# A Mamba-2 branch on one core: the skip term through the decay matrix, the diagonal products of two chunks in one run, and a new place for the last four squares

## The chip, the cores and the metric

The kernel runs on one core of a Trainium2 chip. A core has five engines that run their own instruction streams side by side: TensorE (PE) for matrix products, with its weight loads shown apart (PEld), VectorE (DVE), ScalarE (ACT), GpSimd (POOL) and SyncE (SP), which here only issues transfers. They wait for each other through semaphores. The metric is the device time of one execution in microseconds (us); the time of a kernel is the median of its runs.

## What is computed

One layer of a diffusion backbone on 512 latent tokens of width 1024, with 256 context tokens: a modulated norm, one wide projection, a bidirectional Mamba-2 branch and a windowed attention beside it, gates, an output projection, and a gated convolutional feed-forward part. The change lies in the Mamba-2 branch (4 groups of 8 heads of 64, state 128, chunks of 128 tokens) and in what follows it:

```python
# ssd_scan, one direction
cb = jnp.einsum('bclgn,bcsgn->bgcls', cc, bc)
scores = cb[:, :, None] * jnp.exp(segsum(ac))
y_diag = jnp.einsum('bgrcls,bcsgrp->bclgrp', scores, xc)
y_off = jnp.einsum('bclgn,bcgrpn,bgrcl->bclgrp', cc, states[:, :-1], jnp.exp(cs))
# ssd_output
y = y + d_skip.reshape(SSD_GROUPS, SSD_HPG, 1).astype(y.dtype) * xs
return rmsnorm(y.reshape(Bsz, L, D_SSD) * jax.nn.silu(z), g)
```

The forward and the backward scan are added, so each chunk of a group has one 128 x 128 matrix a head for what its own tokens give each other, two products with the states that come from the left and from the right, and a skip term: its inputs times a number for each head and token (the diagonal that the two directions share, and `d_skip`).

## The kernel before

The program is one long list of steps. A runner goes through it and loads each step's weights one step ahead: SP issues the transfer (L177), ACT makes the rounded part (L183) and DVE the rest (L184), and each product of a projection is three passes on PE (L238, L239, L241). Small pieces of other work are put between a projection's passes through a list, BETWEEN. A scheduler settles the static order of each engine from the program; operations that are recorded as kept in program order stay in it, and on POOL that holds for nearly all of them: the helpers `gp` (L1574) and `gs` (L1577) record it.

For each group, `ssd_steps` gives a step for the states and, for each of the chunks c = 0 to 3, `chunk_in` and `chunk_out`:

- *States.* `advance` takes a state one chunk on: a product on PE (L1597), a decay on POOL (`st<-st,eT`), a sum on DVE (L1600). The states from the right are made first, one behind another, and one of them is needed in chunk 0.
- *chunk_in.* The product `cb` (PE L1696); its diagonal `cbd` (DVE L1698); the skip's coefficients `coef` (POOL); for c > 0 two tiles `dg`, the coefficients on a diagonal (POOL). Then the decay matrices E, two tiles of four heads: ACT L1719, L1722 and L1726, DVE L1723; E times `cb` (DVE L1730); and for c > 0 `E + dg` (POOL), by which the skip goes through the same product as the rest.
- *chunk_out.* Two products with the states (PE L1754, eight matmuls, 16 passes in the trace), each scaled into a tile `te` (DVE L1756); the diagonal products (PE L1762, eight matmuls whose results are 64 columns wide, again 16 passes); the forward state's `advance`; and `y`, the sum of the two `te` (POOL). For c = 0 the skip is a product `dx` on POOL, which four transposes on PE (L1778) add to the diagonal products' bank.
- *late.* Some steps later: the next chunk's decays are loaded, `y` gets the diagonal part (DVE L1779), and the gate `zs` is multiplied in (POOL, for chunk 3 DVE L1783). For groups 1 to 3, squares of the group before are summed (ACT L1570, POOL L1571).

The E tiles come from three buffers, the products' banks (`mis`) from a common pool. After the last chunk of a group its four gated tiles are stored (`yz_d`, SP L1798).

Behind group 3 stands the output projection of this branch. `y_split(ks)` reloads rows of `yz_d` (SP L1840), splits each into a rounded part `yh` (ACT L1842) and a rest `yl` (DVE L1843). The first five rows are of earlier groups. The four tiles of group 3 are squared and summed here, in `square(True)`, from a list. One of the projection's weights is held in a tile that is called `yh` as well (its number is 7766 in the rows below; L183 writes it), and so is PE's operand of the last split.

The step list from which this part comes starts with

```python
[([], lambda: (y_split(range(8)), square(True), square(True), y_split([8, 9]), square(True), square(True), y_split([10, 11])))]
```

Of the kernel before, what the change touches and what calls it, by code (L numbers as in the profile page):

```python
# [9 lines left out]
F32 = mybir.dt.float32  # L10
# [3 lines left out]
ALU = mybir.AluOpType  # L14
# [4 lines left out]
P = 128  # L19
# [20 lines left out]
def raw(ap):  # L40
    return ap.bitcast(F32)
# [3 lines left out]
def tile_hybrid_layer(  # L45
# [32 lines left out]
    V, S, G, T = nc.vector, nc.scalar, nc.gpsimd, nc.tensor  # L78
# [3 lines left out]
    hpool = ctx.enter_context(tc.tile_pool(name="hpool", bufs=1))  # L82
# [27 lines left out]
    def misb():  # L110
        return bank("mis")
# [32 lines left out]
    for j, t in enumerate((wdn[0], DSUMS[1], DSUMS[2], DSUMS[5], DSUMS[4], wdn[1], wdn[3])):  # L144
        for u in range(DU):
            n = min(2, DK - 2 * u) * HC
# [99 lines left out]
    ident = cpool.tile([P, P], F32, name="ident")  # L246
# [181 lines left out]
    with tc.tile_pool(name="spool", bufs=1) as sp:  # L428
# [177 lines left out]
        def square(x_, q, n, k, x):  # L606
            sq = B_[x, k] = tmp(("ta", "tb")[k % 2])[:, :n] if k else q
            S.activation(sq, x_[:, k, :], AF.Square)
# [57 lines left out]
        for j in range(KT):  # L666
# [46 lines left out]
            x = ("hi", "lo") if j >= NU else ("hh", "hl")  # L713
# [31 lines left out]
        for n in range(2):  # L745
            for j in range(KT):
                x = ("hi", "lo") if j >= NU else ("hh", "hl")
# [668 lines left out]
    zp = zpool.enter_context(tc.tile_pool(name="zpool", bufs=1, side="right", reuse_waits="tile"))  # L1416
    bp = bpool.enter_context(tc.tile_pool(name="bpool", bufs=1, reuse_waits="tile"))
# [18 lines left out]
    def h8(a):  # L1436
        return a.rearrange("p (h d) -> p h d", h=8)

    def bc64(a):
        return a.unsqueeze(2).to_broadcast([P, 8, 64])  # L1440
# [132 lines left out]
    def gp(*a):  # L1573
        return tc.keep_in_program_order(G.tensor_tensor(*a))  # L1574
# [4 lines left out]
    def ssd_steps(g):  # L1579
        d = GR[g]  # L1580
# [96 lines left out]
        def chunk_in(c):  # L1677

            if not g and not c:
                far_in(0)  # L1680
            fb = []
            for dr in range(2):
                f = bp.tile([P, 8, P], F32, tag="fb", name="fb", bufs=4)
                a = bass.AP(
                    tensor=cs_d.tensor, offset=cs_d.offset + (32 * dr + 8 * g) * L + c * P, ap=[[0, P], [L, 8], [1, P]]
                )
                dma = nc.sync.dma_start(f, a)
                if not g and not c:
                    tc.add_manual_dep(dma.ins, M_LOADS["x", 16].ins.name, QUEUED, reason="decays behind a projection's weights")
                fb.append(f)  # L1690
            d["E"] = []

            def products():
                cb = d["cb"] = misb()
                tok = slice(c * P, (c + 1) * P)
                T.matmul(cb[:, :P], d["BT"][:, tok], d["CT"][:, tok], start=True, stop=True)  # L1696
                cbd = bp.tile([P, 1], F32, tag="cbd", name="cbd", bufs=2)
                V.tensor_tensor_reduce(  # L1698
                    cb[:, P : 2 * P], cb[:, :P], ident, op0=ALU.mult, op1=ALU.add, scale=1.0, scalar=0.0, accum_out=cbd
                )  # L1700
                coef = d["coef"] = bp.tile([P, 8], F32, tag="coef", name="coef", bufs=2)
                gs(coef, TT[:, c, 8 * g : 8 * g + 8], cbd, None, ALU.mult)
                gp(coef, coef, bcs[:, 8 * g : 8 * g + 8], ALU.add)
                d["dg"] = [diagonal(q) for q in range(2)] if c else None

            def diagonal(q):
                dg = bp.tile([P, 4, P], F32, tag="dg", name="dg", bufs=2)
                w = d["coef"][:, 4 * q : 4 * q + 4].unsqueeze(2).to_broadcast([P, 4, P])
                gp(dg, ident.unsqueeze(1).to_broadcast([P, 4, P]), w, ALU.mult)
                return dg  # L1710

            def decays():
                for q in range(2):
                    E = bp.tile([P, 4, P], F32, tag="E", name="E", bufs=3)
                    eb = misb()
                    F4 = fb[0][:, 4 * q : 4 * q + 4, :]
                    for u in range(4):
                        h = 8 * g + 4 * q + u
                        e0 = S.activation(E[:, u, :], F4[:, u, :], AF.Identity, bias=TX[:, c, 0, h : h + 1])  # L1719
                        if u == 0 and c:  # L1720
                            tc.keep_in_program_order(e0)
                        S.activation(eb[:, u * P : (u + 1) * P], fb[1][:, 4 * q + u, :], AF.Identity, bias=TX[:, c, 1, h : h + 1])  # L1722
                    V.copy_predicated(E, sel.unsqueeze(1).to_broadcast([P, 4, P]), eb.rearrange("p (h l) -> p h l", h=4))  # L1723
                    d["E"].append(E)
                for E in d["E"]:
                    S.activation(flat(E), flat(E), AF.Exp)  # L1726

            def weighed():
                for q, E in enumerate(d["E"]):
                    V.tensor_tensor(E, E, d["cb"][:, :P].unsqueeze(1).to_broadcast([P, 4, P]), ALU.mult)  # L1730
                    if c:
                        gp(E, E, d["dg"][q], ALU.add)

            if g in BY_BLOCKS and not c:
                decays()
                BETWEEN[1:2] = [lambda f=BETWEEN[1]: (f(), products(), weighed())]
            else:
                products()
                decays()
                weighed()  # L1740
            if g and c > 1:
                square()
            if g < 3 and c == 3:
                far_in(0, g + 1)

        def chunk_out(c):
            xs, E, far = d["xs"], d["E"], d.pop(("far", c))
            tok = slice(c * P, (c + 1) * P)
            parts = []
            for dr, s in ((0, d["Sf"]), (1, d["Sb"][c])):  # L1750
                ps = misb()
                for ct in range(4):
                    z = slice(ct * P, (ct + 1) * P)
                    T.matmul(ps[:, z], s[:, z], d["CT"][:, tok], start=True, stop=True)  # L1754
                t = tmp("te")
                V.tensor_tensor(t, ps, flat(far[:, dr]), ALU.mult)  # L1756
                parts.append(t)

            yd = misb()
            for h in range(8):  # L1760
                o = yd[64 * (h % 2) : 64 * (h % 2) + 64, (h // 2) * P : (h // 2 + 1) * P]
                T.matmul(o, xs[:, c, h * 64 : (h + 1) * 64], E[h // 4][:, h % 4, :], start=h < 2, stop=c > 0 and h > 5)  # L1762
            dx = None
            if not c:
                dx = zp.tile([P, 512], F32, tag="th", name="dx", bufs=1)
                gp(h8(dx), h8(xs[:, c, :]), bc64(d["coef"]), ALU.mult)
            if c < 3:
                d["Sf"] = advance(d["Sf"], 0, c, weigh_in(0, c))
            y = bp.tile([P, 512], F32, tag="tf", name="y", bufs=1)
            gp(y, parts[0], parts[1], ALU.add)  # L1770

            def late():

                if c < 3:
                    far_in(c + 1)
                for ct in range(0 if c else 4):
                    z = slice(ct * P, (ct + 1) * P)
                    tc.keep_in_program_order(T.matmul(yd[:, z], dx[:, z], ident, start=False, stop=ct == 3, is_transpose=True))  # L1778
                tc.keep_in_program_order(V.tensor_tensor(y, yd, y, ALU.add))  # L1779
                z = d["zt"][:, :, tok]  # L1780
                x = y.rearrange("p (a t) -> p a t", a=4)
                if c == 3:
                    V.tensor_tensor(z, x, z, ALU.mult)  # L1783
                else:
                    gp(z, x, z, ALU.mult)
                if g and c in (0, 3):
                    square()

            assert not BETWEEN
            if g < 3:  # L1790
                BETWEEN.extend([lambda: None] * 4 + [lambda: (late(), turn(1)), turn])
            else:
                BETWEEN.extend([lambda: None] * 2 + [late])
# [43 lines left out]
    def y_split(ks):  # L1837
        for k in ks:
            t = tmp("ta" if k < 3 else "tc") if k < 5 else ldt[k % 3] if k % 6 < 3 else cp.tile([P, L], F32, tag="ld", name="ld", bufs=3)
            nc.sync.dma_start(t, yz_d[k])  # L1840
            h, l = yh[k // 4][:, k % 4, :], yl[k // 4][:, k % 4, :]
            S.activation(h, t, AF.Copy, scale=col(V_SG, k))  # L1842
            V.scalar_tensor_tensor(l, t, col(V_SG, k), raw(h), ALU.mult, ALU.subtract)  # L1843
# [462 lines left out]
    def down_step(j, u):  # L2306
# [36 lines left out]
        return [("dn", DU * j + u + n) for n in range(4 if tail else 1)], fn  # L2343

    run(
        [([], lambda: (y_split(range(8)), square(True), square(True), y_split([8, 9]), square(True), square(True), y_split([10, 11])))]
        + fill[n3:]
        + [([], zpool.close), os_first(0), ([], lambda: y_split(range(12, 16))), os_first(1)]
        + [os_step(2)]
# [96 lines left out]
```

## Time and profile before

| | |
|---|---|
| median of 3 runs | 1215.3 us (1214.98 to 1215.76) |
| profiled execution | 1215.35 us, its span 1213.6 us |
| granted clock of PE | 0.999 |
| PE | 1203.6 us busy, 99% |
| DVE | 918.6 us, 76% |
| ACT | 684.4 us, 56% |
| POOL | 263.8 us, 22% |

Group 0's four chunks begin near 440 us, group 3's near 667 us, and the first split of a reloaded row is at 722 us. A row of a timeline gives the start, the length, the engine, the line, the operation with the tiles that it writes and reads, how many instructions the row holds, and in brackets how long the engine had been idle before it and what it then waited for. A row of the chain gives the start, the share of time that this piece had on the chain, and its engine and line. A row of waits gives the engine and line that waited, for what, the total in us, how often, and the longest.

### The profile page before, as it was taken

The numbers are of one execution on the slowest core, as the hardware profiler recorded it, in microseconds if no ns is written. First come the engines' busy times: TensorE is split into PE (matmuls) and PEld (weight loads), VectorE is DVE, ScalarE is ACT, GpSimd is POOL, SyncE is SP. The second block draws the span as 40 slices with busy tenths as digits, with TensorE's granted clock in tenths as the row PEclk, the third lists the DMA queues.
The fourth block names the chain that finished last, engine by engine and source line by source line (L and its number), as shares of the span: only waits on it lengthen the run. The fifth ranks groups of instructions, "written<-read, shape, count | busy, mean of one in ns | idle before, by whom it ended". The sixth has DMA issues, their size and how long they took to land.

```text
span 1213.6 us, 17847 instructions
## 1 busy us (share of the span) xinstructions
PE 1203.6 (99%) x6429; PEld 1005.6 (83%) x6429; DVE 918.6 (76%) x1476; ACT 684.4 (56%) x1269; POOL 263.8 (22%) x274
## 2 busy tenths in 40 slices
PE   9999999999999999999999999999999999999998
PEld 6798888888878878788787887888988888888886
DVE  4857887888565588788887978677677767668787
ACT  4557887778543467476575664223544343436654
POOL 0000121100102546264382762000200100110021
PEclk9999999999999999999999999999999999999999
DMA  9655889844747737566477668687266634437662
GB/s 367 253 148 185 161 229 271 170 133 139 170 140 240 228 113 199 157 162 192 145 178 264 176 228 265 221 251 242 50 163 148 195 117 138 130 107 226 213 185 97
DMA packets 129417, 224.30 MB, mean 185 GB/s; under 512 B 27336, under 2 KB 70640, under 8 KB 129328
## 3 DMA queue, kind: packets, MB, share of 16 engines
q1 hardware_dynamic: 115248, 195.61, 52.0%
q0 software_dynamic: 13792, 27.27, 10.1%
q8 instruction: 51, 0.84, 0.3%
q14 instruction: 38, 0.31, 0.1%
q10 hardware_dynamic: 288, 0.27, 0.1%
HBM read 196.17 MB, written 45.02 MB: 199 GB/s over the span
## 4 chain that ended last, share of the span: by engine, by line
PE 90%; DMA 3%; DVE 2%; POOL 2%; issue 1%; ACT 1%; SPq 0%; DVEq 0%; POOLq 0%; ACTq 0%
PE acc L241 18%; PE acc L238 18%; PE acc L239 18%; PE score L979 3%; PE po L1028 3%; PE pt L1015 2%; PE mis L582 2%; PE mis L1754 2%; PE mis L1597 2%; PE mis L2304 2%; PE mis L2302 2%; PE mis L2303 2%; DMA xs_d<-xb 1%; PE acc L2304 1%; PE acc L2302 1%
## 5 line engine op out<-in xcount | busy, mean ns | idle before, releaser
L184 DVE TENSOR_TENSOR wlo<-wraw,whi 128x1024 fp32r<-128x1024 f32 (+1 forms) x115 | 148.3, 1289 | 89.2 <-ACT whi L183 88.3
L183 ACT CAST whi<-wraw 128x1024 fp32r<-128x1024 f32 (+1 forms) x115 | 120.2, 1046 | 154.2 <-PE acc L239 103.4
L238 PE MATMUL acc<-hlh,whi 128*128 128x512 f32 x472 | 192.8, 409 | 0.0
L241 PE MATMUL acc<-hlh,wlo 128*128 128x512 f32 x472 | 185.6, 393 | 0.0
L239 PE MATMUL acc<-hll,whi 128*128 128x512 f32 x472 | 185.0, 392 | 0.0
L238 PE MATMUL acc<-mh,whi 128*128 128x512 f32 x368 | 143.3, 389 | 0.0
L239 PE MATMUL acc<-ml,whi 128*128 128x512 f32 x368 | 143.2, 389 | 0.0
L241 PE MATMUL acc<-mh,wlo 128*128 128x512 f32 x368 | 143.2, 389 | 0.0
L241 PEld LDWEIGHTS acc<-hlh,wlo 128*128 128x128 f32 x472 | 88.6, 188 | 19.9 <-issue 0.5
L238 PEld LDWEIGHTS acc<-hlh,whi 128*128 128x128 f32 x472 | 88.8, 188 | 17.6 <-issue 2.8
L239 PEld LDWEIGHTS acc<-hll,whi 128*128 128x128 f32 x472 | 88.9, 188 | 17.4 <-issue 2.2
L238 PEld LDWEIGHTS acc<-mh,whi 128*128 128x128 f32 x368 | 69.1, 188 | 14.4
L241 PEld LDWEIGHTS acc<-mh,wlo 128*128 128x128 f32 x368 | 69.1, 188 | 14.3
L239 PEld LDWEIGHTS acc<-ml,whi 128*128 128x128 f32 x368 | 69.1, 188 | 14.2
L164 POOL DMA_DIRECT2D dsum<-wdn x24 | 25.3, 1118 | 194.3 <-DVE wlo L1112 183.7
L988 DVE CUSTOM_DVE_ANT_0 p<-score,winm,nsink 128x512 f32<-128x512 f32 (+1 forms) x64 | 51.8, 810 | 15.3 <-PE score L979 13.8
L995 ACT ACTIVATE p<-p,mneg 128x512 f32<-128x512 f32 (+1 forms) x64 | 49.7, 777 | 15.4 <-DVE mneg L988 14.9
L813 DVE SCALAR_TENSOR_TENSOR tm<-wraw,csil,tm 128x512 f32<-128x512 f32 x56 | 45.9, 819 | 13.1 <-DMA wraw<-wm 12.4
L1023 DVE TENSOR_TENSOR ptl<-pt,pth 128x512 fp32r<-128x512 f32 x72 | 47.5, 685 | 8.4 <-ACT pth L1019 7.7
L238 PE MATMUL acc<-hch,whi 128*128 128x256 f32 x176 | 53.2, 302 | 0.0
L1112 DVE TENSOR_TENSOR wlo<-wraw,whi 128x1024 fp32r<-128x1024 f32 x30 | 36.7, 1223 | 18.3 <-ACT whi L1109 18.2
L241 PE MATMUL acc<-hch,wlo 128*128 128x256 f32 x176 | 49.8, 283 | 0.0
(458 smaller groups left out, 3054.3 us busy)
## 6 DMA issues: line engine op xcount, KB each, us to landing
wraw<-wup SPq DMA_DIRECT2D x44, 512.0 KB, 4.0
dsum<-wdn POOLq DMA_DIRECT2D x24, 704.0 KB, 8.7
wraw<-wm SPq DMA_DIRECT2D x32, 512.0 KB, 4.1
fb<-cs_d SPq DMA_DIRECT2D x32, 512.0 KB, 7.5
wraw<-wx SPq DMA_DIRECT2D x24, 512.0 KB, 4.1
wm<-wm SPq DMA_DIRECT2D x16, 512.0 KB, 7.9
wraw<-wz SPq DMA_DIRECT2D x16, 512.0 KB, 4.7
far<-us_d SPq DMA_DIRECT2D x32, 256.0 KB, 5.1
```

What stands on the lines that cost most here:

```text
L183: F["cast"] = S.copy(hi[:, :n], r[:, :n])
L184: F["sub"] = V.tensor_tensor(lo[:, :n], r[:, :n], raw(hi[:, :n]), ALU.subtract)
L238: T.matmul(ps, wh, xh[:, k0 + k, :], start=a, stop=False)
L239: T.matmul(ps, wh, xl[:, k0 + k, :], start=False, stop=False)
L241: T.matmul(ps, wl, xh[:, k0 + k, :], start=False, stop=b)
L813: V.scalar_tensor_tensor(acc, r[:, u * 512 : u * 512 + 512], sc, acc, ALU.mult, ALU.add)
L988: V.tensor_tensor_reduce(p[:, :w], d["ps"][i][:, o0 : o0 + w], m, op0=ALU.add, op1=ALU.min, scale=1.0, scalar=nsink[:, h : h + 1], accum_o ...
L995: S.activation(p, p, AF.Exp, bias=d["mneg"][:, i : i + 1], scale=-1.0, accum_out=d["den"][:, i : i + 1])
L1023: V.tensor_tensor(d["ptl"][x], d["pt"][x], raw(d["pth"][x]), ALU.subtract)
L1112: sum_step(V.tensor_tensor(d["w"][1], d["r"], raw(d["w"][0]), ALU.subtract), 1 + (4 <= g < 12))
L2302: T.matmul(ps, h, wh, start=st, stop=False, skip_group_check=True)
L2304: T.matmul(ps, h, wl, start=False, stop=en, skip_group_check=True)
```

## The change

The skip of chunk 0 goes the way of the others: `dg` and `E + dg` are made for every chunk, and `dx` and the four transposes of L1778 are gone. The diagonal products of chunk 0, and in groups 0 to 2 also of chunk 2, are not done in their own `chunk_out`, but in the next chunk's, in one run of sixteen matmuls with that chunk's own. Since a held chunk's E lives longer, an odd chunk's second E tile comes from another pool, and a held chunk's `y` too. The sum of `y` and the gate's product are then done for both chunks in the later one's `late`. In group 3, chunks 2 and 3 keep a run each. The last four squares, which stood two by two between the splits of rows 8 to 11, now all stand behind the first five splits.

```diff
-                d["dg"] = [diagonal(q) for q in range(2)] if c else None
+                d["dg"] = [diagonal(q) for q in range(2)]
...
-                    E = bp.tile([P, 4, P], F32, tag="E", name="E", bufs=3)
+                    if c % 2 and q:
+                        E = hpool.tile([P, 4, P], F32, tag="rbc4", name="E")
+                    else:
+                        E = bp.tile([P, 4, P], F32, tag="E", name="E", bufs=3)
...
-                    if c:
-                        gp(E, E, d["dg"][q], ALU.add)
+                    gp(E, E, d["dg"][q], ALU.add)
...
-            yd = misb()
-            for h in range(8):
-                o = yd[64 * (h % 2) : 64 * (h % 2) + 64, (h // 2) * P : (h // 2 + 1) * P]
-                T.matmul(o, xs[:, c, h * 64 : (h + 1) * 64], E[h // 4][:, h % 4, :], start=h < 2, stop=c > 0 and h > 5)
-            dx = None
-            if not c:
-                dx = zp.tile([P, 512], F32, tag="th", name="dx", bufs=1)
-                gp(h8(dx), h8(xs[:, c, :]), bc64(d["coef"]), ALU.mult)
+            held = c == 0 or c == 2 and g < 3
+            d.setdefault("held", []).append((c, E))
+            done = []
+            for n, Es in [] if held else d.pop("held"):
+                yd = misb()
+                for h in range(8):
+                    o = yd[64 * (h % 2) : 64 * (h % 2) + 64, (h // 2) * P : (h // 2 + 1) * P]
+                    T.matmul(o, xs[:, n, h * 64 : (h + 1) * 64], Es[h // 4][:, h % 4, :], start=h < 2, stop=h > 5)
+                done.append((n, yd))
...
-            y = bp.tile([P, 512], F32, tag="tf", name="y", bufs=1)
+            y = hpool.tile([P, 512], F32, tag="q2", name="y") if held else bp.tile([P, 512], F32, tag="tf", name="y", bufs=1)
             gp(y, parts[0], parts[1], ALU.add)
+            d["y", c] = y
...
-                for ct in range(0 if c else 4):
-                    z = slice(ct * P, (ct + 1) * P)
-                    tc.keep_in_program_order(T.matmul(yd[:, z], dx[:, z], ident, start=False, stop=ct == 3, is_transpose=True))
-                tc.keep_in_program_order(V.tensor_tensor(y, yd, y, ALU.add))
-                z = d["zt"][:, :, tok]
-                x = y.rearrange("p (a t) -> p a t", a=4)
-                if c == 3:
-                    V.tensor_tensor(z, x, z, ALU.mult)
-                else:
-                    gp(z, x, z, ALU.mult)
+                for n, yd in done:
+                    y = d.pop(("y", n))
+                    tc.keep_in_program_order(V.tensor_tensor(y, yd, y, ALU.add))
+                    z = d["zt"][:, :, n * P : (n + 1) * P]
+                    x = y.rearrange("p (a t) -> p a t", a=4)
+                    if n == 3:
+                        V.tensor_tensor(z, x, z, ALU.mult)
+                    else:
+                        gp(z, x, z, ALU.mult)
...
-        [([], lambda: (y_split(range(8)), square(True), square(True), y_split([8, 9]), square(True), square(True), y_split([10, 11])))]
+        [([], lambda: (y_split(range(5)), [square(True) for _ in range(4)], y_split(range(5, 12))))]
```

The lines behind L1704 move by up to 3 in the changed kernel: L1754 becomes L1756, L1762 becomes L1768, L1779 becomes L1782, L1842 becomes L1845.

The order on POOL, group 3, from chunk 0's coefficients to its `y`, before:

```order
L1577 TENSOR_SCALAR coef<-TT,cbd 128x8
L1574 TENSOR_TENSOR coef<-coef,bcs 128x8
L1574 TENSOR_TENSOR st<-st,eT 128x512 x2
L1574 TENSOR_TENSOR dx<-xs,coef 128x512
L1574 TENSOR_TENSOR st<-st,eT 128x512
L1574 TENSOR_TENSOR y<-te 128x512
```

and now:

```order
L1577 TENSOR_SCALAR coef<-TT,cbd 128x8
L1574 TENSOR_TENSOR coef<-coef,bcs 128x8
L1574 TENSOR_TENSOR dg<-ident,coef 128x512 x2
L1574 TENSOR_TENSOR E<-E,dg 128x512 x2
L1574 TENSOR_TENSOR st<-st,eT 128x512 x3
L1574 TENSOR_TENSOR y<-te 128x512
```

Two `dg` and two sums into E stand ahead of the states, and `dx` is gone. On PE, in the same place, chunk 0's eight products with the states are now four, four projection passes, and four more, and the 64-column run of chunk 0 is gone.

The order on DVE, group 3, between chunk 1 and chunk 2, from chunk 1's two `te` to chunk 2's E (`y` is the sum with the diagonal part, `tm` and `mod` belong to the modulation's small sums, `g1h` to the output gate), before:

```order
L1756 TENSOR_TENSOR te<-mis,far 128x512 x2
L811 TENSOR_SCALAR tm<-wraw,csil 128x512
L1600 TENSOR_TENSOR st<-st,mis 128x512
L1698 ISA mis,cbd<-mis,ident 128x128
L1698 ISA cbd 128x1
L1779 TENSOR_TENSOR y<-mis,y 128x512
L813 SCALAR_TENSOR_TENSOR tm<-wraw,csil,tm 128x512
L1723 COPY_PREDICATED E<-sel,mis 128x512 x2
L813 SCALAR_TENSOR_TENSOR tm<-wraw,csil,tm 128x512
L1730 TENSOR_TENSOR E<-E,mis 128x512 x2
```

and now:

```order
L1758 TENSOR_TENSOR te<-mis,far 128x512 x2
L1782 TENSOR_TENSOR y<-mis,y 128x512 x2
L811 TENSOR_SCALAR tm<-wraw,csil 128x512
L1600 TENSOR_TENSOR st<-st,mis 128x512
L1698 ISA mis,cbd<-mis,ident 128x128
L1698 ISA cbd 128x1
L813 SCALAR_TENSOR_TENSOR tm<-wraw,csil,tm 128x512
L1977 TENSOR_SCALAR g1h<-mod_94 128x8
L813 SCALAR_TENSOR_TENSOR tm<-wraw,csil,tm 128x512
L1726 COPY_PREDICATED E<-sel,mis 128x512 x2
L813 SCALAR_TENSOR_TENSOR tm<-wraw,csil,tm 128x512
L1733 TENSOR_TENSOR E<-E,mis 128x512 x2
```

Both `y` sums stand ahead of the state sum and of chunk 2's `cbd`, and one more `tm` and `g1h` ahead of E.

The order on ACT behind group 3, from the last split of an earlier group's row on (`yh_7766` written by L183 is the second weight of the output projection, `whi` the other weights, `ta` the squares), before:

```order
L1842 ACTIVATE yh_7768<-tc,vec 128x512
L778 ACTIVATE tb<-acc 128x512
L183 CAST whi<-wraw 128x1024
L183 CAST yh_7766<-wraw 128x1024
L1842 ACTIVATE yh_7768<-ld,vec 128x512
L1842 ACTIVATE yh_7768<-ld_7762,vec 128x512
L183 CAST whi<-wraw 128x1024
L1842 ACTIVATE yh_7768<-ld_7763,vec 128x512
L1570 ACTIVATE ta<-zs 128x512 x2
```

and now:

```order
L1845 ACTIVATE yh_7768<-tc,vec 128x512
L778 ACTIVATE tb<-acc 128x512
L1570 ACTIVATE ta<-zs 128x512 x4
L183 CAST whi<-wraw 128x1024
L1845 ACTIVATE yh_7768<-ld,vec 128x512
L183 CAST yh_7766<-wraw 128x1024
L1845 ACTIVATE yh_7768<-ld_7762,vec 128x512
L1845 ACTIVATE yh_7768<-ld_7763,vec 128x512
L1845 ACTIVATE yh_7770<-ld_7764,vec 128x512
```

The four squares stand together behind the earlier groups' splits, and the second weight's cast stands behind the split of the first reloaded row instead of ahead of it.

## The prediction

> **What bounds the kernel now.** I read the shares of busy time first, then the waits of TensorE, then the chain of work that ended last.
>
> ```profile
> span 1213.6 us, 17847 instructions
> PE 1203.6 (99%) x6429; PEld 1005.6 (83%) x6429; DVE 918.6 (76%) x1476; ACT 684.4 (56%) x1269; POOL 263.8 (22%) x274
> PE 90%; DMA 3%; DVE 2%; POOL 2%; issue 1%; ACT 1%; SPq 0%; DVEq 0%; POOLq 0%; ACTq 0%
> PE acc L241 <- DVE wlo L184: 1.3, 1, 1.3
> ```
>
> PE is busy 99% of the span and the chain lies on it for 90%, so a pass taken off PE is time saved, and a wait given to PE is time lost. The last row is PE's longest wait, the only one over 1.0 us. Both sides of the change meet in the stretch where the chain leaves PE:
>
> ```profile
> 671.99 0.23 PE acc L241
> ...
> 681.78 0.45 PE mis L1778 x4
> ...
> 706.66 2.51 POOL E L1574 x2
> 709.17 2.23 POOL ssq L1571
> ...
> 714.80 1.06 DVE zs L1783
> ...
> 719.68 4.06 DMA ld<-yz_d
> ...
> 735.48 1.14 DVE wlo L184
> 736.63 0.04 issue
> 736.67 0.50 PE acc L241
> ```
>
> From 682 to 737 us the chain runs over POOL, DVE, SP and ACT: group 3's decay matrices, the gate, the trip through memory and the row splits, up to the weight for which PE waits. POOL is busy 22% over the span, but in this stretch it is what sets the end.
>
> **What PE saves.** One run of the diagonal products, in group 0:
>
> ```profile
> 440.47 1.95 PE L1754 MATMUL mis<-CT,st 128*128 128x128 f32 x16
> 442.35 1.09 PE L1762 MATMUL mis<-E,xs 128*64 128x128 f32 x16
> 443.38 1.12 PE L1597 MATMUL mis<-xw,Bk 128*128 128x512 f32 x2
> L1754 PE MATMUL mis<-CT,st 128*128 128x128 f32 x256 | 31.2, 275 | 0.0
> L1762 PE MATMUL mis<-E,xs 128*64 128x128 f32 x256 | 17.5, 279 | 0.0
> ```
>
> With one pass at 0.275 us, the last L1754 pass starts at 440.47 + 1.95 - 0.275 = 442.145, so its sixteen are (442.145 - 440.47) / 15 = 0.112 apart; the first L1762 pass comes 0.205 after it, 0.09 more than that spacing. L1762's last pass starts near 443.165 (0.279 before its end), so its sixteen are 0.054 apart, and L1597 comes 0.215 after the last, 0.16 more. Entering and leaving a 64-column run costs **about 0.25 us** in all. The sixteen passes of the second chunk cost the same 0.87 wherever they stand.
>
> The change leaves 9 of the 16 runs: two go in each of groups 0 to 2, one in group 3. The four transposes of L1778 (0.45 in the chain's row) go in every group. Groups 0 to 2: 3 x (0.45 + 2 x 0.25) = **2.85 us saved**. Group 3: 0.45 + 0.25 = 0.70. What the change puts in their place in groups 0 to 2 (two `dg`, two sums into E on POOL, less the product `dx`) I cost at nothing: the products of a held chunk wait for the next chunk's own E, which POOL finishes later than the held one, and between the chunks lie projections on PE. If that cover were gone, one group would lose about 3.5 us of POOL work (2.04 + 2.54 - 1.04, rows below).
>
> **What group 3 loses.** Here the projections between the chunks are few. Times are in the clock of the trace, without the 2.85 us by which all of it comes earlier.
>
> ```profile
> 667.83 1.07 POOL L1574 TENSOR_TENSOR st<-st,eT 128x512 f32<-128x512 f32 x1
> 669.70 1.06 POOL L1574 TENSOR_TENSOR st<-st,eT 128x512 f32<-128x512 f32 x1 [0.80 <-DVE st L1600]
> 670.72 1.04 POOL L1574 TENSOR_TENSOR dx<-xs,coef 128x512 f32<-128x512 f32 x1
> ...
> 678.57 2.04 POOL L1574 TENSOR_TENSOR dg<-ident,coef 128x512 f32<-128x512 f32 x2
> 680.57 2.54 POOL L1574 TENSOR_TENSOR E<-E,dg 128x512 f32<-128x512 f32 x2
> 683.09 1.27 POOL L1574 TENSOR_TENSOR zs<-y,zs 128x512 f32<-128x512 f32 x1
> ...
> 687.93 1.40 POOL L1574 TENSOR_TENSOR y<-te 128x512 f32<-128x512 f32 x1 [0.34 <-DVE te L1756]
> ...
> 689.98 2.49 POOL L1574 TENSOR_TENSOR dg<-ident,coef 128x512 f32<-128x512 f32 x2
> 694.24 3.01 POOL L1574 TENSOR_TENSOR E<-E,dg 128x512 f32<-128x512 f32 x2 [1.76 <-DVE E L1730]
> ...
> 699.49 2.26 POOL L1574 TENSOR_TENSOR zs<-y,zs 128x512 f32<-128x512 f32 x1
> 701.70 1.06 POOL L1574 TENSOR_TENSOR st<-st,eT 128x512 f32<-128x512 f32 x1
> ```
>
> *Chunk 0.* Before, the two state steps start at 667.83, right behind the coefficients. Now the order puts two `dg` and two sums into E ahead of them: 667.9 + 2.04 + 2.54 = 672.5, then state 1.06, DVE's sum (0.68, row below), state 1.06, sum 0.68: about 676.0. PE comes to the run at 672.06, does the first four products (0.9), four projection passes (0.23 each), and wants the last state at 673.9. It **waits about 2.2 us**, between 1.5 (if DVE is quicker) and 3 (if `dg` and E take the 2.49 and 3.01 of the later rows). Nothing hides it: the four passes are all that stands between.
>
> *Chunk 1.* POOL's `y` follows the late products, near 678.7; then coefficients, `dg`, E to about 685.6, against 683.1. The gate product `zs` (1.27) has left this place, so the square sum ends near 687.9, the state at 688.9, and the `y` of chunk 1 at 690.3, against 689.34.
>
> *Chunk 2.* DVE's order now matters:
>
> ```profile
> 688.10 0.68 DVE L1600 TENSOR_TENSOR st<-st,mis 128x512 f32<-128x512 f32 x1
> 688.70 0.28 DVE L1698 CUSTOM_DVE_ANT_0 mis<-mis,ident 128x128 f32<-128x128 f32 x1
> ...
> 689.36 0.69 DVE L1779 TENSOR_TENSOR y<-mis,y 128x512 f32<-128x512 f32 x1 [0.32 <-POOL y L1574]
> ...
> 693.39 1.27 DVE L1730 TENSOR_TENSOR E<-E,mis 128x512 f32<-128x512 f32 x2
> ...
> 696.01 1.26 DVE L1974 TENSOR_SCALAR g1h<-mod 128x8 f32<-128x8 f32 x1
> ```
>
> Before, the sum `y` stood behind the diagonal of chunk 2's product (L1698), and only `y` waited for POOL. Now both `y` sums stand ahead of the state sum and of that diagonal, and queue them behind POOL's `y` at 690.3: sum 0.69, one scaling of 0.5, state sum 0.68, diagonal 0.35, so 692.5 in place of 689.0, **3.5 us later**. From that diagonal to POOL's E it was 694.24 - 689.0 = 5.2. Of these, `y` with its wait (1.0) goes, and `g1h` (1.26) and one more scaling step (0.7) stand in its place: 6.2. POOL's E starts near 698.8, 4.6 later than before.
>
> *Chunk 3.* E 2.5 to 3.0, square sum 2.2, now two `zs` in place of one (1.27 to 2.26 each), state 1.06; from the state's end at 702.76 to the end of chunk 3's E at 709.17 it was 6.4, and these steps keep their order. With E 2.5, one `zs` short and one between, the E of chunk 3 ends near 714.5 (bounds 713 and 716) in place of 709.17.
>
> ```profile
> 708.92 1.09 PE L1762 MATMUL mis<-E,xs 128*64 128x128 f32 x16
> ...
> 723.01 0.39 PE L238 MATMUL acc<-yh,yh 128*128 128x512 f32 x1
> 717.16 1.05 ACT L183 CAST yh<-wraw 128x1024 fp32r<-128x1024 f32 x1
> 722.49 0.72 ACT L1842 ACTIVATE yh<-ld,vec 128x512 fp32r<-128x512 f32 x1 [4.28 <-DMA ld<-yz_d]
> 720.22 1.21 DVE L184 TENSOR_TENSOR yh<-wraw,yh 128x1024 fp32r<-128x1024 f32 x1
> ```
>
> Before, PE takes the second half of chunk 3's run at 708.92 + 8 x 0.054 = 709.4, only 0.2 after POOL has it ready. There was no slack, so from here PE is late by 714.5 - 709.4 = **5.1 us**, whatever it lost at chunk 0 and gained from its own 0.70.
>
> *The row splits.* The second output weight (the `yh` written by L183) was cast at 717.16, before the first reload arrived at 722.45. Now it stands behind the split of that reload. The reload came 13.3 us after chunk 3's E (722.45 - 709.17), along gate, store and load, and these keep their order. So cast 13.3 + 0.7 + 1.05 = 15.05, DVE's part 1.21 more: 16.3. PE wants the first at 723.01 - 709.17 = 13.8 and the second 0.46 later; counted from E it waits 1.25, then 0.8: **2.05 us** new. Against it goes the wait of 1.3 at 736.67: the four squares with their sums on POOL now end before the later splits, which on DVE need no more than their uncontended length. If that cover fails, the 1.3 stays.
>
> **Sum.** -2.85 + 5.1 + 2.05 - 1.3 = **+3.0**. On the profiled execution (1215.35 with what lies around its span, level with the median 1215.3) this is 1218.3. With E's bounds of 713 and 716, it is 1216.8 to 1219.8. The change breaks even where chunk 3's E ends at 711.5.
>
> **Rivals.**
>
> *The slip is swallowed and the saving shows (faster).* If POOL and DVE have enough gaps to bring chunk 3's E in by 709.5, the sum is -2.85 + 2.05 - 1.3 = -2.1, so 1213.2, and without the new wait at the splits -2.85 - 1.3, so 1211.2. For it speaks POOL's idle time in the rows (0.80, 0.34 and 1.76); against it that chunk 0's addition of 3.5 us stands ahead of a state for which PE has four passes of cover, and that the last of the gaps is behind DVE, which is itself moved later. 1211.0 to 1213.5.
>
> *About even.* If the square sum of chunk 1 takes the short length and POOL's `y` ends near 688.9, the diagonal of chunk 2 is 2.1 and not 3.5 later; with both `zs` short, E ends between 711.5 and 713: 1215.3 to 1216.8.
>
> *A longer loss (slower).* The same POOL operations have two lengths in the rows: `dg` 2.04 and 2.49, E 2.54 and 3.01, `zs` 1.27 and 2.26, the long ones beside DVE work from SBUF. If the added ones are all long, chunk 2's E ends at 702.5 and chunk 3's at 702.5 + 2.2 + 2 x 2.26 + 1.06 + 6.4 = 716.7, and the sum gives 1220.5; with the long wait at chunk 0 feeding into it, up to 1222. [...]
>
> *The run's overhead is not a matter of runs.* If the 0.25 belongs to each chunk's products and not to the run, seven runs fewer save nothing: 6 x 0.25 = 1.5 us of the saving goes, 1219.8.
>
> **How the numbers follow.** Forecast 0.50, spread over 1216.8 to 1219.8; even 0.22; faster 0.12; longer loss 0.11; overhead stays 0.05. Predicted 1218.3. About 0.2%, 2.4 us, is what a measurement of this kernel can tell from no change: under 1212.9 is faster, over 1217.7 slower. Slower: two thirds of the forecast (0.34) and the two last rivals, 0.50. Same: the rest of the forecast, the even case and a little of the faster one, 0.39. Faster 0.11. The range of 8 in 10 leaves out the faster case below 1213 and the upper end of the longer loss: 1213.0 to 1221.0.
>
> **What would show it.** In the profile after: no L1778 rows and about 0.45 + 0.5 us less PE time in each of groups 0 to 2, with no new waits there; a PE wait of about 2 us on a state (L1600) in group 3; E of chunk 3 from POOL some 5 us later against the run before it, with a PE wait of 2 to 3 us on it; a wait on the second output weight of about 2 us, and none at the third and fourth. I am wrong if PE does not wait at group 3's last diagonal run, or if the waits arise in groups 0 to 2.

## The result and the profile after

The changed kernel takes 1230.92 us (median of 4 runs, 1229.6 to 1231.95) against 1215.53 us beside it: a ratio of 1.0126, 95% interval 1.0114 to 1.0138. It is 15.4 us slower. The direction was forecast, the size was not: 3 us were forecast, and the range ended at 1221.0. Two executions that took far longer than the others of their kernel (3380.73 us with group 3 alone changed, 1336.17 us of the kernel before) are left out of the ratios below.

The page of the changed kernel, the rows that answer to the first ones of before:

```profile
span 1227.8 us, 17812 instructions
PE 1204.4 (98%) x6413; PEld 1005.8 (82%) x6413; DVE 916.8 (75%) x1476; ACT 685.5 (56%) x1269; POOL 276.5 (23%) x286
PE 82%; DVE 6%; DMA 3%; POOL 3%; ACT 2%; issue 2%; DVEq 0%; POOLq 0%; ACTq 0%; SPq 0%
```

PE's share of the chain fell from 90% to 82%; what it lost went above all to DVE (2% to 6%), the rest to POOL, ACT and issue. POOL has 12.7 us more work. The waits of PE in the changed kernel (what waited, for what; us in total, times, longest):

```profile
PE mis L1768 <- POOL E L1574: 3.9, 3, 2.1
PE mis L1756 <- DVE st L1600: 3.1, 1, 3.1
PE mis L1597 <- ACT xsc L1549: 2.9, 2, 1.7
PE mis L1450 <- DVE tc L1431: 1.5, 3, 0.7
PE mis L1756 <- ACT xsc L1549: 1.2, 1, 1.2
PE mis L1616 <- DVE xw L1585: 1.1, 1, 1.1
...
PE mis L1696 <- DVE te L1758: 0.8, 1, 0.8
PE mis L1756 <- ACT xs L1549: 0.6, 1, 0.6
PE acc L241 <- DVE wlo L184: 0.6, 1, 0.6
PE acc L241 <- DVE yh L184: 0.5, 1, 0.5
```

The first two rows and the last two are group 3 and the row splits, where waits were forecast. Nearly all others lie in groups 0 to 2, where none was. (The wait on `xw` is not the change's: it stands ahead of group 0's first chunk and is 0.4 us in the kernel before, 0.4 to 1.1 in the runs below with five banks.) To split the loss in place, take the first sum of context states in group 3. In the timeline of before it stands at

```profile
656.13 1.88 PE L1616 MATMUL mis<-xw,Bkc 128*128 128x512 f32 x4
```

and in that of the changed kernel at

```profile
662.24 1.88 PE L1616 MATMUL mis<-xw,Bkc 128*128 128x512 f32 x4
```

So groups 0 to 2, which should have brought 2.85 us, cost 6.1, and the other 8.1 of the 14.2 us by which the spans differ come from group 3 on. The profiled execution is the fastest of the four.

**Groups 0 to 2.** PE in the changed kernel, group 1, chunk 2, with what follows in chunk 3:

```profile
548.21 1.13 PE L1756 MATMUL mis<-CT,st 128*128 128x128 f32 x8 [0.65 <-ACT xs L1549]
550.56 1.16 PE L1756 MATMUL mis<-CT,st 128*128 128x128 f32 x8 [1.22 <-ACT xsc L1549]
551.56 1.02 PE L1597 MATMUL mis<-xw,Bk 128*128 128x512 f32 x2
...
563.51 1.97 PE L1768 MATMUL mis<-E,xs 128*64 128x128 f32 x32
```

and the same chunk 2 in the kernel before:

```profile
545.16 1.95 PE L1754 MATMUL mis<-CT,st 128*128 128x128 f32 x16
547.13 1.09 PE L1762 MATMUL mis<-E,xs 128*64 128x128 f32 x16
548.16 1.12 PE L1597 MATMUL mis<-xw,Bk 128*128 128x512 f32 x2
```

The sixteen passes went through in one piece; now each half waits until ACT has copied `xs` or `xsc`. Those copies empty the banks of the transposes (L1450) just ahead, and have nothing to do with the states in content. It is the bank that is wanted. Each program fixes the bank of every result when it is built, and these numbers say the same for this place:

```
bank wanted in chunk 2 by    before: last filled by          changed: last filled by
state product 1              product cb (L1696)              transposes for xs (L1450)
state product 2              transposes for xs (L1450)       transposes for xsc (L1450)
diagonal products            transposes for xsc (L1450)      no bank wanted here
next state (L1597)           chunk 1's diagonal products     chunk 0's diagonal products
```

Five banks serve all of this. The run of chunks 0 and 1 fills two of them, where chunk 1's run filled one, and both are kept until the late sums, several pieces later. Three are left, and each product of chunk 2 gets a bank that was filled one product later than the one it used to get: the first the bank of `xs`, the second that of `xsc`, filled just ahead. The waits of `L1597` for `xsc` in groups 0 and 2 stand at the same kind of place. Together the waits for copies are 4.7 us; the 0.8 for `te` is for a bank as well. The 0.7 for `tc` ahead of groups 2 and 3 is not: `tc` is what the transposes read.

**Group 3.** POOL in the changed kernel:

```profile
674.05 2.49 POOL L1574 TENSOR_TENSOR dg<-ident,coef 128x512 f32<-128x512 f32 x2
676.51 2.98 POOL L1574 TENSOR_TENSOR E<-E,dg 128x512 f32<-128x512 f32 x2
...
705.34 2.52 POOL L1574 TENSOR_TENSOR E<-E,dg 128x512 f32<-128x512 f32 x2 [3.21 <-DVE E L1733]
...
718.48 3.48 POOL L1574 TENSOR_TENSOR E<-E,dg 128x512 f32<-128x512 f32 x2
```

and DVE between chunks 1 and 2:

```profile
697.00 0.69 DVE L1782 TENSOR_TENSOR y<-mis,y 128x512 f32<-128x512 f32 x1 [1.72 <-POOL y L1574]
...
698.60 0.30 DVE L1698 CUSTOM_DVE_ANT_0 mis<-mis,ident 128x128 f32<-128x128 f32 x1
...
699.47 0.17 DVE L1977 TENSOR_SCALAR g1h<-mod 128x8 f32<-128x8 f32 x1
701.07 1.61 DVE L813 SCALAR_TENSOR_TENSOR tm<-wraw,csil,tm 128x512 f32<-128x512 f32 x1 [1.43 <-DMA wraw<-wm]
```

Less the 6.1 us of the groups ahead, chunk 2's diagonal is done at 698.9 - 6.1 = 692.8 (forecast 692.5), POOL's E of chunk 2 starts at 699.2 (698.8), and chunk 3's E ends at 721.96 - 6.1 = 715.9 (714.5, bounds 713 and 716). The order on DVE did what was said of it. What comes behind was not foreseen. PE at chunk 3's run in the changed kernel:

```profile
719.80 0.66 PE L1768 MATMUL mis<-E,xs 128*64 128x128 f32 x8 [2.10 <-POOL E L1574]
722.01 0.66 PE L1768 MATMUL mis<-E,xs 128*64 128x128 f32 x8 [1.55 <-POOL E L1574]
...
722.98 0.63 PE L239 MATMUL acc<-hll,whi 128*128 128x512 f32 x1
723.40 0.63 PE L241 MATMUL acc<-hlh,wlo 128*128 128x512 f32 x1
```

and the table of two stretches (PE busy, PEld, DVE, ACT, POOL, then the granted clock, the share of DMA and GB/s):

```profile
719.80:728.00 8.20, 6.65 (x33) 5.11 (x34) 4.38 (x6) 3.69 (x6) 7.14 (x5) 0.79 0.40 137
700.00:708.00 8.00, 8.00 (x45) 6.85 (x43) 5.54 (x7) 4.65 (x9) 4.71 (x6) 1.00 0.69 192
```

After two waits of 2.10 and 1.55 us with little between, projection passes start 0.42 us apart in place of 0.23. From 724 to 726 us the granted clock is 0.50: the clock had been halved, and eight to nine passes lost about 0.2 us each, 1.6 us in all.

### The profile page after: what moved, and what is told of

It is laid out like the page before. It is cut to its first block, busy times and chain, and to the rows that moved or that the text cites. A ratio compares the mean times of both kernels' runs of the same rounds, so it can differ in the third digit from the quotient of the medians.

```text
span 1227.8 us, 17812 instructions
## 1 busy us (share of the span) xinstructions
PE 1204.4 (98%) x6413; PEld 1005.8 (82%) x6413; DVE 916.8 (75%) x1476; ACT 685.5 (56%) x1269; POOL 276.5 (23%) x286
## 4 chain that ended last, share of the span: by engine, by line
PE 82%; DVE 6%; DMA 3%; POOL 3%; ACT 2%; issue 2%; DVEq 0%; POOLq 0%; ACTq 0%; SPq 0%
PE acc L241 16%; PE acc L238 16%; PE acc L239 16%; PE score L979 3%; PE po L1028 3%; PE pt L1015 2%; PE mis L582 2%; PE mis L2306 2%; PE mis L2307 2%; PE mis L2305 2%; PE acc L2306 1%; PE acc L2307 1%; PE acc L2305 1%; PE acc L1098 1%; PE acc L1100 1%
## 5 line engine op out<-in xcount | busy, mean ns | idle before, releaser
L184 DVE TENSOR_TENSOR wlo<-wraw,whi 128x1024 fp32r<-128x1024 f32 (+1 forms) x115 | 151.3, 1317 | 93.4 <-ACT whi L183 90.1
L183 ACT CAST whi<-wraw 128x1024 fp32r<-128x1024 f32 (+1 forms) x115 | 120.1, 1045 | 152.0 <-PE acc L239 98.6
L239 PEld LDWEIGHTS acc<-ml,whi 128*128 128x128 f32 x368 | 69.1, 188 | 14.2
L238 PEld LDWEIGHTS acc<-mh,whi 128*128 128x128 f32 x368 | 69.1, 188 | 14.2
L988 DVE CUSTOM_DVE_ANT_0 p<-score,winm,nsink 128x512 f32<-128x512 f32 (+1 forms) x64 | 51.9, 810 | 15.4 <-PE score L979 13.9
L995 ACT ACTIVATE p<-p,mneg 128x512 f32<-128x512 f32 (+1 forms) x64 | 49.7, 777 | 15.4 <-DVE mneg L988 14.8
L1725 ACT ACTIVATE mis<-fb,TX 128x128 f32<-128x128 f32 x128 | 41.7, 357 | 14.9 <-DVE te L1758 7.0
```

The costliest lines, as they stand in the source:

```text
L183: F["cast"] = S.copy(hi[:, :n], r[:, :n])
L184: F["sub"] = V.tensor_tensor(lo[:, :n], r[:, :n], raw(hi[:, :n]), ALU.subtract)
L238: T.matmul(ps, wh, xh[:, k0 + k, :], start=a, stop=False)
L239: T.matmul(ps, wh, xl[:, k0 + k, :], start=False, stop=False)
L988: V.tensor_tensor_reduce(p[:, :w], d["ps"][i][:, o0 : o0 + w], m, op0=ALU.add, op1=ALU.min, scale=1.0, scalar=nsink[:, h : h + 1], accum_o ...
L995: S.activation(p, p, AF.Exp, bias=d["mneg"][:, i : i + 1], scale=-1.0, accum_out=d["den"][:, i : i + 1])
```

## The experiments

All times are read against the kernel before on the same chip; ratios have their 95% intervals, and the us are worked out from the ratios. Of each edit the lines that decide are shown; lines that follow from them are left out.

**The parts alone.** The first three undo all but one part. Groups 0 to 2 changed alone:

```diff
-            held = c == 0 or c == 2 and g < 3
+            held = g < 3 and c in (0, 2)
...
-                d["dg"] = [diagonal(q) for q in range(2)]
+                d["dg"] = [diagonal(q) for q in range(2)] if (c or g < 3) else None
```

> The changed kernel with group 3 and the squares as they were before: skip through E and runs of two chunks in groups 0 to 2 alone. Theory on record (no wait in these groups): 2.85 us faster than before, 1212.6. New theory (two result banks are held from the long run until the late sums, three of five banks are left for the transposes, products and states, and PE waits for ACT and DVE to empty them): the changed kernel's trace stands 6.0 us behind before where group 3 begins, so about 1221.5.

Measured: 1.0056 (1.0039 to 1.0073), 6.8 us slower, median 1222.12, with the same waits for `xs` and `xsc` at the same places as in the changed kernel. The banks' theory said 6; the forecast on record fell here. Group 3 alone:

```diff
-            held = c == 0 or c == 2 and g < 3
+            held = g == 3 and c == 0
```

> The kernel before with group 3 alone changed (skip of chunk 0 through E, chunk 0 and 1 in one run), squares as before. Theory on record: chunk 3's E 5.1 us late, and the wait of 1.3 at the row splits stays, so 5 us slower, 1220.5. New theory adds: group 3's bank waits are few, most of the 8.3 us that the changed kernel loses from group 3 on is POOL's chain: 1220 to 1224.

Measured: 1.0066 (1.0049 to 1.0082), 8.0 us slower, inside the new theory's range. The state's wait is 3.1, E's waits are 2.36 and 1.55, and the passes behind them start 0.43 apart, the spacing that the changed kernel has at a granted clock of 0.50. The squares alone, in the kernel before:

```diff
-y_split(range(8)), square(True), square(True), y_split([8, 9]), square(True), square(True), y_split([10, 11])
+y_split(range(5)), [square(True) for _ in range(4)], y_split(range(5, 12))
```

> The kernel before with the four squares behind the first five splits and nothing else. Theory on record: the wait of 1.3 goes, a wait of 2.05 on the second output weight comes: 0.75 us slower, 1216.1. Rival: the changed kernel waits only 1.1 us at the splits, so no slower than before: 1214 to 1215.3.

Measured: 1.0012 (1.0003 to 1.0021), 1.5 us slower. A new wait came, as forecast, but at the first weight and not the second; in this run PE's waits begin with

```profile
PE acc L241 <- DVE wlo L184: 2.0, 1, 2.0
```

and DVE ahead of it ran long, beside the square sums on POOL that now stand there:

```profile
717.61 3.49 DVE L1843 SCALAR_TENSOR_TENSOR yl<-tc,vec,yh 128x512 fp32r<-128x512 f32 x2
721.02 2.29 DVE L184 TENSOR_TENSOR wlo<-wraw,whi 128x1024 fp32r<-128x1024 f32 x1
```

The two splits took 1.40 in the kernel before, the weight 1.21. Part of the 1.5 us goes with the granted clock: five of the ten executions have a granted clock of 0.999 to 1.000 and take 1216.0 on average, 0.7 us above the mean of the kernel before; five have 0.997 and take 1217.4 to 1217.6. The profiled one is of these, and 1.5 us behind its wait its passes stand 0.43 apart for 3 us. The parts sum to 16.3 us, the whole is 15.4.

**Are the banks the cause?** First the late sums, which empty the two banks, right behind the long run:

```diff
+            early = g < 3 and len(done) == 2
...
-                BETWEEN.extend([lambda: None] * 4 + [lambda: (late(), turn(1)), turn])
+                adds = [lambda a=a: add(*a) for a in done] if early else []
+                BETWEEN.extend(adds + [lambda: None] * (4 - len(adds)) + [lambda: (late(), turn(1)), turn])
```

> The changed kernel, but in groups 0 to 2 the two sums that empty the result banks of a long run stand two and three pieces earlier, right behind it, and the gate's products where they were. Bank theory: PE's waits for the copies xs and xsc in groups 0 to 2 (4.7 us) go, and with them others: 1223 to 1226.5. If the waits come from ACT's or POOL's own load and not from banks: 1230 to 1231, as the changed kernel.

Measured: 1.0152 (1.0137 to 1.0167), 18.5 us slower: no gain, and above both ranges. The trace tells why; its group 3 begins with

```profile
658.17 1.88 PE L1616 MATMUL mis<-xw,Bkc 128*128 128x512 f32 x4
666.01 3.33 PE L1616 MATMUL mis<-xw,Bkc 128*128 128x512 f32 x4 [3.88 <-DVE xw L1585]
```

At the first row it is 4.1 us ahead of the changed kernel (662.24), and no wait on `xs` or `xsc` over 0.2 us is left. Then it loses all of it at once: the order had moved a modulation step ahead of `xw` on DVE, and that step waits 6.86 us for its weights. From there on the passes start 0.42 to 0.43 us apart three times in this trace (behind the wait of 3.88, one of 3.1 and one of 1.55), once in the changed kernel's. At the first row it is still 2.0 us behind the kernel before (656.13), and not 2.85 ahead: the waits for copies are 4.1 us of the loss, not all of it. With group 3 and the squares as before, the same edit:

> Groups 0 to 2 changed, the two late sums of a long run right behind it, group 3 and squares as before. Bank theory: the waits for xs and xsc are gone, 4 us less than the run with these groups changed, 1217.5 to 1219. If the wait of 3.9 us on xw that the earlier run with early sums showed at group 3's start comes back (a weight load in front of xw on DVE): 1222 to 1224.

Measured: 1.0078 (1.0063 to 1.0093), 9.5 us slower, median 1224.28; the weight load came back in DVE's way (a wait of 6.04 us) and hides the gain from the total. At group 3's first row this trace is 3.3 us ahead of the run with these groups changed (658.84 against 662.14), as the bank theory has it. So the sums' place settles the waits for banks, not the time. Next, the number of banks alone:

```diff
-    psum_pools(mis=(5, 1), acc=(3, 1))
+    psum_pools(mis=(6, 1), acc=(2, 1))
```

once with groups 0 to 2 changed, once in the kernel before. In groups 0 to 2 POOL's order stays as it was, and PE's but for group 0's first steps; the scheduler moves some instructions on DVE and ACT, in both kernels.

> Groups 0 to 2 changed as in that run, with six banks for the transposes, products and states and two for the projections in place of five and three. To be read against the next run. Bank theory: at most 2 us behind it (4 to 7 us less than the 7 between the same two kernels with five banks), and no PE wait on the copies xs and xsc. If banks are not the cause: 6 to 8 us behind it.

> The kernel before with six and two banks. Every theory: the projections lose by two banks, by 0 to 10 us; it is the measure for the run ahead of it.

Measured: 1.0144 (1.0127 to 1.016) and 1.0134 (1.0119 to 1.0149), medians 1233.18 and 1231.53. Both pay some 16 us for having two projection banks, more than the 10 allowed for, but nearly all of it behind group 3's start: there the kernel before with six banks is at 656.73, with five at 656.13. The difference between the two medians, 1.65 us, is what the change in groups 0 to 2 costs with six banks; with five it was 6.8. The executions overlap (1232.22 to 1234.56 against 1230.93 to 1232.85), so the 1.65 is barely told from nothing, but not from 6.8. The traces say the same: at group 3's first row 657.63 against 656.73, 0.9 apart, where with five banks it is 662.14 against 656.13, 6.0 apart. The waits left in groups 0 to 2 of the former are

```profile
PE mis L1696 <- ACT xsc L1549: 1.0, 1, 1.0
PE mis L1450 <- DVE tc L1431: 0.8, 1, 0.8
PE mis L1597 <- ACT xsc L1549: 0.4, 1, 0.4
```

So most of the loss goes with one bank more. In the place of the table above the two state products have their old fillers again, the product `cb` and the transposes for `xs`, and don't wait. Even then these groups bring no gain; 1.4 us of the waits that are left are again for a copy, where the theory had none. With the `tc` waits (0.8, and 0.7 ahead of group 3) that is about the 2.85 that should have shown.

**Which half brings them?** The skip through E without long runs, and long runs without it, in groups 0 to 2:

```diff
-            held = g < 3 and c in (0, 2)
+            held = False
```

> Groups 0 to 2 with the skip of chunk 0 through E, but each chunk's diagonal products in a run of their own and summed as before; group 3 and squares as before. If the waits in these groups come from the two result banks that a long run holds: none of them here, and the transposes' 3 x 0.44 go, 1213.8. If they come from POOL's added work (dg and E of chunk 0): as with the whole change in these groups, 1218 to 1222.

Measured: 1.0075 (1.006 to 1.009), 9.1 us slower, more than either theory had. As the bank theory says, no wait on a copy is left, but PE waits on E, 4.9 us in five places, and most in group 0:

```profile
447.11 0.77 PE L1770 MATMUL mis<-E,xs 128*64 128x128 f32 x8 [3.18 <-POOL E L1574]
448.34 1.12 PE L1770 MATMUL mis<-E,xs 128*64 128x128 f32 x8 [0.47 <-POOL E L1574]
449.39 1.81 PE L1597 MATMUL mis<-xw,Bk 128*128 128x512 f32 x2
```

(the last row is 1.81 us against 1.12 in the prediction's rows). Chunk 0's E is too late for a run of its own; what hides POOL's work in the changed kernel is the holding, as the prediction said. The waits and the longer rows behind them are some 6 of the 9.1 us; the rest was not pursued. And the long runs alone:

```diff
-                d["dg"] = [diagonal(q) for q in range(2)] if (c or g < 3) else None
+                d["dg"] = [diagonal(q) for q in range(2)] if (c > 0) else None
```

> Groups 0 to 2 with runs of two chunks, but chunk 0's skip by dx and four transposes as before; group 3 and squares as before. Bank theory: all the waits stay, and the transposes too, 1222 to 1224. If the waits come from POOL's added work: 1213 to 1214 (six runs fewer, 0.25 to 0.35 us each).

Measured: 1.0095 (1.008 to 1.011), 11.5 us slower, median 1226.56, above the range. It waits 3.2 us for `xs` in two places, so the copies' waits belong to the long runs. It has further waits in group 2 (1.5 on a product into E by DVE, 1.5 on a state) that the changed kernel has not; where these come from was not pursued.

**Group 3, order by order.** On POOL, chunk 0's states ahead of its `dg` and E:

```diff
-                    if (c or g == 3):
+                    if c:
                         gp(E, E, d["dg"][q], ALU.add)
+                if g == 3 and not c:
+                    def skip_in():
+                        for q, E in enumerate(d["E"]):
+                            gp(E, E, diagonal(q), ALU.add)
+                    BETWEEN.append(skip_in)
```

> Group 3 alone changed, squares as before, and on POOL the two states of chunk 0 ahead of its dg and its sums into E. The wait of 3.1 us on the state goes in either case. If it also set the rest of the chain (PE's place, the weight load that DVE waits for in chunk 2): chunk 3's E comes 2.5 to 3 us earlier than in the run with group 3 changed, and the waits before it are too short for the clock to drop: 1218.5 to 1220.5. If chunk 2's order on DVE alone sets it: 1222.5 to 1224.

Measured: 1.0039 (1.0024 to 1.0054), 4.7 us slower, 3.3 less than group 3 changed alone. The state's wait is gone, and chunk 3's E ends 2.4 us earlier (713.44 against 715.84); at that E one wait of 1.05 is left. But the spacing of 0.23 was not kept: the run of chunks 0 and 1 now waits 1.55 us on E, and behind that wait alone the passes start 0.42 apart, for as long as in the run with group 3 changed; the granted clock is 0.998 in each of the four executions, against 0.999 to 1.000 of the kernel before. That the waits before E would be too short for this was the author's estimate; no run shows such a length. On DVE, chunk 2's diagonal ahead of the late sums:

```diff
+                    if g == 3 and c == 1:
+                        tc.add_manual_dep(added.ins, d["cbd"].ins.name, QUEUED, reason="late sums behind the next chunk's product")
```

> Group 3 alone changed, squares as before, and on DVE chunk 2's diagonal (cbd) ahead of the two late sums of chunks 0 and 1. Theory on record (the late sums hold the diagonal back by up to 3.5 us): chunk 3's E 2 to 3.5 us earlier, 1219.5 to 1221.5. If a weight load that DVE waits for behind it covers most of that: at most 1 us earlier, 1222 to 1223.5.

Measured: 1.0054 (1.0037 to 1.0071), 6.6 us slower, 1.4 less than group 3 changed alone, an amount that the intervals don't separate from none; in the trace chunk 3's E ends 1.5 us earlier (714.36), between what the two theories had. Both:

> Group 3 alone changed, with chunk 0's states ahead on POOL and chunk 2's diagonal ahead on DVE. If the two are separate parts of the chain's delay, their gains add up (4.0 and 2.3 us off the run with group 3 changed): 1217 to 1218. If one covers the other: 1219 to 1220.

Measured: 1.0025 (1.0014 to 1.0035), 3.0 us slower. By the ratios the gains are 3.3 and 1.4 alone and 5.0 together, but the median, 1218.33, lies between the two ranges on record: whether the gains add up stays open. With both, the changed group 3 still loses.

No variant that was run beats the kernel before: groups 0 to 2 gain nothing even with a bank more, and group 3 loses in every order tried. Early sums with the modulation step kept behind `xw` on DVE were not run.

## Why the prediction was wrong

*The term for groups 0 to 2: the step that failed.* The prediction put the additions there "at nothing", and named one cover only, that a held chunk's E is not needed until the next run. That cover holds: without the holding PE waits for E. What it did not ask is what holding itself keeps busy. A long run fills two of five banks until the late sums. In place of -2.85 the term is +6.1 by the traces: 4.7 us of waits for copies and 0.8 for `te`, all for banks. With a sixth bank, groups 0 to 2 cost 1.65 us in place of 6.8. What is left of the term (the waits for `tc` among it) has no shown cause. The bank numbers of the two programs, which need no run, had the main part in sight: the products of the next chunk wait for other instructions than they did.

*What PE saves: right, a little small.* Changed kernel, group 0, chunk 0:

```profile
440.90 1.95 PE L1756 MATMUL mis<-CT,st 128*128 128x128 f32 x16
442.68 1.02 PE L1597 MATMUL mis<-xw,Bk 128*128 128x512 f32 x2
```

From the first state product to L1597 it is 1.78 us, against 443.38 - 440.47 = 2.91 before, and sixteen more passes in a run cost 1.97 - 1.09 = 0.88: a run saves 0.25 as forecast. L1597's row is 0.1 shorter here as well (1.02 against 1.12), so it may be a little more. The rival that the overhead is not a matter of runs is out.

*Chunk 0 in group 3: right in place, small.* 2.2 us were forecast, with 3 if POOL takes the long lengths; it took them (2.49 and 2.98) and the wait is 3.1. The run with the states first shows that this stall is not absorbed by the later one, as the prediction had it ("whatever it lost at chunk 0"): taking it away gains 3.3 us in the total. In the traces 2.4 of these are chunk 3's E: chunk 2's diagonal comes 1.15 us earlier, and the weights that DVE then waits for come 2.5 us earlier (the `tm` behind them starts at 693.36 in place of 695.83).

*Chunk 3's E: right within its bounds* (715.9 in before's clock, bounds 713 and 716), by the steps that were given, with one difference inside: `g1h` took 0.17 and not 1.26, and a wait of 1.43 for weights stands in its place. E itself took the long length, 3.48.

*The clock: missing.* The prediction had PE late by E and left it at that. The half clock behind the two waits (granted 0.50 from 724 to 726 us) cost a further 1.6 us. The runs don't tie it to the length of the wait. Passes 0.42 to 0.43 us apart came behind single waits of 1.55 us (states first), 1.95 (the squares alone) and 3.1 (early sums). Behind waits of 1.74 and 3.10 in the changed kernel (at 471.55 and 683.23 us) the passes stayed 0.23 apart, at a granted clock of 1.00. The same wait in the same order of PE went both ways: in the run with group 3 changed the eight passes behind it take 1.13 us, in the run with the diagonal ahead of the late sums 2.05.

```profile
676.86 1.13 PE L1757 MATMUL mis<-CT,st 128*128 128x128 f32 x8 [3.09 <-DVE st L1600]
```

```profile
676.92 2.05 PE L1757 MATMUL mis<-CT,st 128*128 128x128 f32 x8 [3.09 <-DVE st L1600]
```

So the length of the wait alone does not decide, and these runs don't show what does. The forecast itself had a wait of 2 to 3 us at E and of 2.2 at chunk 0, and no term for what the clock might do behind them.

*The rivals.* None had the banks. The longer loss (up to 1222) had POOL's long lengths right, as the rows of E and `dg` show, and they are 1 us of chunk 3's E. The faster and the even case needed E by 709.5 and by 713 in before's clock.

*The row splits: right in part, small in effect.* The second weight is waited for 0.5 us in place of 2.05, the old wait of 1.3 is gone as forecast, and a wait of 0.6 on the first weight's rest (`wlo`) came that was not. In the changed kernel the second weight does stand behind the split of the reload:

```profile
734.05 0.72 ACT L1845 ACTIVATE yh<-ld,vec 128x512 fp32r<-128x512 f32 x1
734.68 1.03 ACT L183 CAST yh<-wraw 128x1024 fp32r<-128x1024 f32 x1
```

but the wait for it is shorter. Counted from the end of E (721.96), the cast is done after 13.75 us in place of 15.05, and PE, held up by the clock and by the first weight, comes to it after 16.2 in place of 13.8. In the kernel before with this edit alone the whole wait is on the first weight: DVE's work ahead of it is longer beside the square sums on POOL (3.49 against 1.40 us for two splits).

By the span of the traces: 6.1 for groups 0 to 2, 6.6 for E (715.9 against 709.4 where PE wanted it before), 1.6 for the clock, and the row splits about even (1.1 of new waits against 1.3): 14.3, against 14.2 between the spans.

## What to carry to other kernels

Before costing moved work at nothing, ask for each buffer that it holds longer which later instruction gets the buffer next, and what empties it: here a pair of result banks out of five cost 4.7 us of waits for copies, against the 1.5 us that six runs fewer saved. A wait on PE can cost more than its own length: behind some waits of 1.55 to 3.9 us the passes started 0.42 to 0.43 us apart for a while in place of 0.23 (1.6 us more in the changed kernel, where the granted clock was 0.50), behind others of up to 3.1 they did not, so a difference of a microsecond or two is read with the granted clock of each execution beside it. And an edit that puts sums elsewhere also lets the scheduler put a step that waits for memory ahead of what PE needs next, so the order of the whole engine has to be read, not that of the edited lines alone.

## What was not expected of the hardware

In the changed kernel the half clock (granted 0.50 from 724 to 726 us) lasted for eight to nine projection passes of 0.43 us, after which they were back at 0.23; it cost 1.6 us. Slower passes came behind one wait of 3.09 us (eight state passes in 2.05 us) and not behind another of the same length at the same place (1.13). POOL's sums into E took 1.25 us each in some places and 1.74 in others (2.51 and 3.48 for two), and DVE's splits beside POOL's square sums 1.75 in place of 0.70 each.
